# Gather of expert tokens in groups of two from tokens split once, with the activation transposes moved ahead of the weights' split

## The chip, the cores and the metric

The kernel runs on one core of one Trainium2 chip. The metric is the device time of one execution in microseconds (us). Five engines matter: TensorE (PE in the rows, its weight loads PEld), VectorE (DVE), ScalarE (ACT), GpSimd (POOL) and SyncE (SP), whose queue issues the weight transfers.

## The reference

Two decoder layers over 272 tokens (16 learned ones and 256 of the input) with a width of 1024. Each layer mixes the tokens (a gated convolution beside differential attention) and then applies a channel mixer: dense on layer 0, a mixture of eight experts on layer 1. Only the mixture is touched here:

```python
logits = einsum('bld,de->ble', h, w_router)
top_val, top_idx = lax.top_k(logits, 2)
gate = sum(one_hot(top_idx, 8) * softmax(top_val)[..., None], axis=-2)
for e in range(8):
    out = out + gate[..., e:e+1] * ((silu(h @ w_gate[e]) * (h @ w_up[e])) @ w_down[e])
h = layer_norm(ALPHA * h + out)      # ALPHA = 4 ** 0.25
```

`w_gate` and `w_up` are 1024 x 3584 for each expert, `w_down` 3584 x 1024, all float32, so the experts' weights are 352 MB.

## The kernel before, in words

**Precision.** Products are made in float32r on TensorE. Both operands are split into a float32r part `hi` and a rest `lo = x - hi`, and a product is three matmuls: hi by hi, hi by lo, lo by hi (`wmm`, lines 1020 to 1023). For the weights ScalarE writes `whi` (line 173) and VectorE `wlo` (line 174), one unit of 128 x 2048 (1 MB) at a time.

**Units and buffers.** `Weights` streams the units through raw buffers (six, and NPF = 6 more from layer 1 on; SP issues a load as soon as `wlo` has freed a buffer) and through NSPL = 4 pairs `whi`, `wlo`. `W.fill`, called behind every part (half a unit, six matmuls of 512 columns), splits the next unit when a pair has come free, so ScalarE and VectorE each get one split in every two parts, in program order with all else that they do.

**The loop.** For each of 8 experts and 7 chunks of 512 hidden columns: four gate parts (`gu_part`), the transposes of the activations of the chunk before (`act_T`, line 1038: four transposes on TensorE into a bank `t`, `aTh` on ScalarE, `aTl` on VectorE), four up parts, and four down parts for the chunk before (`down_part`). That is 12 parts, 72 matmuls, six units of weights. `silu` and `times` make the activations. The result of an expert is split (`ysplit`) and scattered to token rows (`scatter`, `scatter_add`) one chunk after its last down part, in the second chunk of the next expert.

**The gather.** Up to 128 tokens of an expert are collected by products with a 0/1 matrix `sel` (`gather_sel`, line 982). In the last chunk of each expert, `gather_k` (line 988) runs for the eight 128-row blocks k of the next expert: two float32 matmuls of 128 columns (four records in the trace, line 992) into a bank `t`, of which there are two; `xg` hi on ScalarE (line 996, with gain and bias); the same value again, `gx`, on VectorE (line 997); and the difference on GpSimd (line 998). The list `ahead` sets behind which part each block runs. The first expert's gather runs before its first parts.

**Order.** The order is written by hand: each engine runs its own instructions in program order. `act_T` stands behind the `W.fill` of the last gate part, so in the queues of ScalarE and VectorE the copies `aTh` and `aTl` stand behind `whi` and `wlo`. The bank `t` of the transposes comes free with `aTl`, and a bank of the gather with `gx`. The tiles of `aT` have four buffers, shared with `ysplit` and, at the start, with four tiles `gb` of gain and bias.

**Residual.** `residual` (line 1102) forms ALPHA * (gain * ht + bias) on GpSimd in `acc`: four multiplies of `gb` by ALPHA (line 1107) and eight `tensor_tensor` (lines 1112 and 1114), in the first chunks of the first expert.

Of the kernel before, what the change touches and what calls it, by code (L numbers as in the profile page):

```python
# [10 lines left out]
F32 = mybir.dt.float32  # L11
# [9 lines left out]
P = 128  # L21
# [9 lines left out]
NCH = DFE // 512  # L31
NRAW = 6
NSPL = 4
NPF = 6
ALPHA = 4.0 ** 0.25
EPS = 1e-5
NEG = -1e30
# [150 lines left out]
def body(tc, h0T, consts, vecs, lamv, w_in, w_out, w_gu, w_dn, w_r, mixgb, w_g, w_u, w_d, out, dbg=None):  # L188
    nc = tc.nc
    with ExitStack() as ctx:  # L190
# [763 lines left out]


        mp = ctx.enter_context(tc.tile_pool(name="moe", bufs=1))
        ht = mp.tile([P, 2, D], F32, name="ht")
        gb = [[mp.tile([P, 512], F32, tag="aT", bufs=4, name=nm("gb")) for n in range(2)] for i in range(2)]
        for i in range(2):
            for n in range(2):  # L960
# [18 lines left out]
        G = {}  # L979
        table(AF.Silu)  # L980

        def gather_sel(e):
            sel = mp.tile([P, 2, P], F32, tag="sel", bufs=1, name=nm("sel"))
            for j in range(2):
                nc.vector.tensor_scalar(sel[:, j], iota, pos[:, j, e:e + 1], None, op0=ALU.is_equal)
            G[e] = (sel, [None] * NK)

        def gather_k(e, k):
            sel, xg = G[e][:2]
            tp = bank("s", 2) if e == 0 and k % 4 > 1 else bank("t", 2)  # L990
            for j in range(2):
                nc.tensor.matmul(tp[:, 0:P], ht[:, j, k * P:(k + 1) * P], sel[:, j], start=(j == 0), stop=(j == 1))
            g, bb = vcol(V_MIX + 16 + k), vcol(V_MIX + 24 + k)
            x = mp.tile([P, P], F32, tag="gx", bufs=2, name=nm("gx"))
            xg[k] = mp.tile([P, 2, P], F32R, tag=f"xg{k}", bufs=1, name=nm("xg"))
            nc.scalar.activation(xg[k][:, 0], tp[:, 0:P], AF.Identity, scale=g, bias=bb)
            nc.vector.tensor_scalar(x, tp[:, 0:P], g, bb, op0=ALU.mult, op1=ALU.add)  # L997
            nc.gpsimd.tensor_tensor(xg[k][:, 1], x, xg[k][:, 0].bitcast(F32), ALU.subtract)  # L998

        def gather_T(e):  # L1000
            sel, xg = G[e][:2]
# [5 lines left out]
            G[e] = (sel, xg, selT)  # L1007

        def gates():
            nc.scalar.activation(ex, ex, AF.Exp)  # L1010
# [14 lines left out]
        def gu_part(o, e, p, sc=False, then=None):  # L1025

            w = W.next()
            xg = G[e][1]
            for k in range(2):
                kk = 2 * p + k  # L1030
                wmm(o, xg[kk][:, 0], xg[kk][:, 1], w.hi[:, k], w.lo[:, k], kk == 0, kk == NK - 1)
# [41 lines left out]
        def scatter(e, n, yh, yl, j):  # L1073
            o = bank("o", 1)
            for i, t in enumerate((yh, yl)):
                nc.tensor.matmul(o, G[e][2][:, j], t, start=i == 0, stop=i == 1)
            scatter_add(e, n, j, o)

        def scatter_add(e, n, j, o):
# [18 lines left out]
        def stats(j, n):  # L1098
            nc.vector.bn_stats(st[:, j, n], acc[:, j, n * 512:(n + 1) * 512])

        gather_sel(0)

        def residual():
            for i in range(2):
                for n in range(2):
                    t = gb[i][n]
                    nc.gpsimd.tensor_scalar(t, t, ALPHA, None, op0=ALU.mult)
                    for j in range(2):
                        ns = slice(n * 512, (n + 1) * 512)
                        a = acc[:, j, ns]  # L1110
                        if i == 0:
                            nc.gpsimd.tensor_tensor(a, ht[:, j, ns], t, ALU.mult)
                        else:
                            nc.gpsimd.tensor_tensor(a, a, t, ALU.add)

        ahead = ((0,), (1,), (2, 3), (4,), (5,), (6,), (7,), ())
        prev, y, pend, act = None, {}, [], None
        for e in range(NE):
            for c in range(NCH):
                end = e == NE - 1 and c == NCH - 1  # L1120
                og = bank()
                pact, act = act, mp.tile([P, 512], F32, tag="act", bufs=2, name=nm("act"))

                def silu():
# [2 lines left out]
                def on_gate(p):  # L1127
                    if e == 0 and c == 0 and p < 2:
                        for k in (4 + 2 * p, 5 + 2 * p):
                            gather_k(0, k)  # L1130
                    if p == 3:
                        silu()

                if e == 0 and c == 0:
                    for k in range(4):
                        gather_k(0, k)
                for p in range(4):
                    gu_part(og, e, p, p % 2, lambda: on_gate(p))
                if prev:
                    aT = act_T(pact)  # L1140
                    pe, pc = prev
                    if pc == 0:
                        y[pe] = [bank("s", 2) for n in range(2)]
# [2 lines left out]
                def times():  # L1146
                    nc.vector.tensor_tensor(act, act, ou, ALU.mult)

                last = c == NCH - 1 and e < NE - 1

                def then(p):
                    if p == 3:
                        times()
                    if last:
                        for k in ahead[p]:
                            gather_k(e + 1, k)

                for p in range(4):
                    gu_part(ou, e, p, p % 2, lambda: then(p))
                    if p == 3 and e < NE - 1 and c == 2:  # L1160
                        gather_sel(e + 1)
                    if p == 3 and e < NE - 1 and c == 4:
                        gather_T(e + 1)
                if end:
                    for n in range(2):
                        for p in range(2):
                            down_part(y[pe], pc, aT, n, p)
                        if n == 0:
                            aT2 = act_T(act)
                    for p in range(2):  # L1170
                        down_part(y[e], c, aT2, 0, p)
                    ys = ysplit(y[e], 0)
                    down_part(y[e], c, aT2, 1, 0)
                    for n in range(2):
                        o = [bank(), bank("o", 1)]
                        for i, j in ((0, 0), (0, 1), (1, 0), (1, 1)):
                            nc.tensor.matmul(o[j], G[e][2][:, j], ys[i], start=i == 0, stop=i == 1)
                        for j in range(2):
                            scatter_add(e, n, j, o[j])
                            if n == 1:  # L1180
                                stats(j, 1)
                                if j == 0:
                                    rstd(0)
                                    for q in ((0, 1), (1, 0), (1, 1)):
                                        final_rows(*q)
                            if n == j == 1:
                                final_scale(0)
                        if n == 0:
                            down_part(y[e], c, aT2, 1, 1)
                            stats(0, 0)  # L1190
                            ys = ysplit(y[e], 1)
                            final_rows(0, 0)
                            stats(1, 0)
                elif prev:
                    for n in range(2):
                        for p in range(2):
                            down_part(y[pe], pc, aT, n, p, (lambda: [gather_k(e + 1, k) for k in ahead[4 + 2 * n + p]]) if last else None)
# [6 lines left out]
                if e == 0 and c == 0:  # L1204
# [5 lines left out]
                if e == NE - 1 and c == NCH - 3:  # L1210
                    finb = W.take()[:, 0:2 * D].rearrange("p (a d) -> p a d", a=2)
                    xo = W.take()[:, 0:D].rearrange("p (k t) -> p k t", k=NK)


        def overflow(e):
# [5 lines left out]
            for k in range(NK):  # L1221
                tp = bank("t", 2)
                ks = slice(k * P, (k + 1) * P)
                for j in range(2):
                    nc.tensor.matmul(tp[:, :P], ht[:, j, ks], sel[:, j], start=(j == 0), stop=(j == 1))
                nc.vector.tensor_scalar(xo[:, k], tp[:, :P], vcol(V_MIX + 16 + k), vcol(V_MIX + 24 + k),
                                        op0=ALU.mult, op1=ALU.add)
# [135 lines left out]
```

## Time and profile before

| | us |
|---|---|
| median of 3 runs | 1555.19 (1549.22 to 1557.51) |
| the profiled execution | 1554.9 |
| its span in the trace | 1553.1 |
| experts' loop, first matmul of line 1021 to the last chunk's end | from 516.53 |
| a chunk without gather or scatter | 16.80 |
| a chunk with the gather of the next expert | 24.38 to 24.91, seven of them |

The span is cut into stretches at the first gate matmul of each chunk, which the timeline of TensorE shows. In a row of stretches the columns are the stretch, its length, the busy time and count of each engine, TensorE's granted clock, the share of the DMA engines and their rate. A timeline row gives start, duration, engine, line, what is written from what, and in brackets the idle time before it and what ended it.

### The profile page before, as it was taken

The page shows a single profiled execution, that of the slowest core. Times are in us where ns is not written, and L with a number is a line of the kernel's source. Part 1 is how long each engine was busy: PE and PEld are TensorE (multiplying, and loading weights), DVE is VectorE, ACT ScalarE, POOL GpSimd, SP SyncE. Part 2 cuts the span into 40 slices and gives each one's busy share as a digit, 9 for nine tenths or more (in the row PEclk, how much of TensorE's full clock was granted, in tenths as well). Part 3 has the DMA queues.
Part 4 walks back from the last instruction along what each step waited for, and adds up shares of the span by engine and source line. Part 5 has one row for each costly group of instructions (what it writes and reads, how often), then busy time and mean ns, then how long its engine had stood idle before and what let it go on. Part 6 is the DMA issues. An engine that isn't in the chain of part 4 may idle for free. (4 is left out here: it accounts for less than half of the span.)

```text
span 1553.1 us, 20974 instructions
## 1 busy us (share of the span) xinstructions
PE 1490.7 (96%) x8181; PEld 1282.5 (83%) x8181; DVE 1244.6 (80%) x1262; ACT 1007.5 (65%) x1105; POOL 134.5 (9%) x169
## 2 busy tenths in 40 slices
PE   9899999999999899999999999999999999999996
PEld 8689899999789778788788788878878878877885
DVE  8767775466866798798799798888879879888886
ACT  6655464445655767677677677767767767777773
POOL 2102200022102630000000000000000000000001
PEclk9899999999999999999999999999999999999998
DMA  8423264354527699899899889979979989997950
GB/s 304 175 82 127 92 228 154 112 189 187 192 82 291 243 358 377 306 359 374 300 358 370 345 322 369 372 295 359 371 298 358 374 316 343 376 366 300 361 207 29
DMA packets 65243, 427.99 MB, mean 276 GB/s; under 512 B 7520, under 2 KB 11616, under 8 KB 15344
## 3 DMA queue, kind: packets, MB, share of 16 engines
q1 hardware_dynamic: 64672, 426.20, 72.6%
q8 instruction: 66, 1.08, 0.3%
q10 hardware_dynamic: 432, 0.35, 0.1%
q14 instruction: 41, 0.34, 0.1%
q0 software_dynamic: 32, 0.03, 0.0%
HBM read 423.27 MB, written 1.05 MB: 273 GB/s over the span
## 5 line engine op out<-in xcount | busy, mean ns | idle before, releaser
L174 DVE TENSOR_TENSOR wlo<-raw,whi 128x2048 fp32r<-128x2048 f32 x332 | 765.8, 2309 | 116.0 <-ACT whi L173 116.0
L173 ACT ACTIVATE whi<-raw 128x2048 fp32r<-128x2048 f32 x332 | 637.8, 1921 | 185.5 <-PE ps L1023 183.9
L1021 PE MATMUL ps<-whi,xg 128*128 128x512 f32 x896 | 357.1, 398 | 0.0
L1023 PE MATMUL ps<-whi,xg 128*128 128x512 f32 x896 | 350.3, 391 | 0.2 <-POOL xg L998 0.2
L1022 PE MATMUL ps<-wlo,xg 128*128 128x512 f32 x896 | 349.6, 390 | 0.0
L284 PE MATMUL ps<-hh,whi 128*128 128x272 f32 (+4 forms) x736 | 220.1, 299 | 6.0 <-ACT hh L393 3.2
L285 PE MATMUL ps<-hl,whi 128*128 128x272 f32 (+4 forms) x736 | 216.1, 294 | 2.8 <-DVE hl L394 2.7
L287 PE MATMUL ps<-hh,wlo 128*128 128x272 f32 (+4 forms) x720 | 210.5, 292 | 2.1 <-DVE wlo L152 2.1
L152 DVE TENSOR_TENSOR wlo<-raw,whi 128x1024 fp32r<-128x1024 f32 (+2 forms) x148 | 171.2, 1179 | 36.4 <-ACT whi L145 36.3
L1023 PEld LDWEIGHTS ps<-whi,xg 128*128 128x128 f32 x896 | 168.5, 188 | 36.8 <-POOL xg L998 0.6
L1022 PEld LDWEIGHTS ps<-wlo,xg 128*128 128x128 f32 x896 | 168.8, 188 | 32.7
L1021 PEld LDWEIGHTS ps<-whi,xg 128*128 128x128 f32 x896 | 168.6, 188 | 32.4
L1021 PE MATMUL ps<-whi,aTh 128*128 128x512 f32 x448 | 177.7, 397 | 0.0
L1023 PE MATMUL ps<-whi,aTl 128*128 128x512 f32 x448 | 175.0, 391 | 2.5 <-DVE aTl L277 2.5
L145 ACT ACTIVATE whi<-raw 128x1024 fp32r<-128x1024 f32 (+2 forms) x148 | 144.9, 990 | 49.0 <-PE ps L285 37.5
L1022 PE MATMUL ps<-wlo,aTh 128*128 128x512 f32 x448 | 174.5, 389 | 0.0
L284 PEld LDWEIGHTS ps<-hh,whi 128*128 128x128 f32 x736 | 142.6, 194 | 8.6 <-ACT hh L393 3.4
L285 PEld LDWEIGHTS ps<-hl,whi 128*128 128x128 f32 x736 | 142.8, 194 | 4.7 <-DVE hl L394 3.5
L287 PEld LDWEIGHTS ps<-hh,wlo 128*128 128x128 f32 x720 | 139.1, 193 | 2.8 <-DVE wlo L152 2.8
L1023 PEld LDWEIGHTS ps<-whi,aTl 128*128 128x128 f32 x448 | 84.1, 188 | 21.5 <-DVE aTl L277 3.8
L998 POOL TENSOR_TENSOR xg<-gx,xg 128x128 fp32r<-128x128 f32 x64 | 28.6, 459 | 841.9 <-DVE gx L997 841.7
L1022 PEld LDWEIGHTS ps<-wlo,aTh 128*128 128x128 f32 x448 | 84.2, 188 | 16.3
(252 smaller groups left out, 1615.4 us busy)
## 6 DMA issues: line engine op xcount, KB each, us to landing
raw<-in_w_g_dram SPq DMA_DIRECT2D x112, 1024.0 KB, 4.9
raw<-in_w_u_dram SPq DMA_DIRECT2D x112, 1024.0 KB, 4.9
raw<-in_w_d_dram SPq DMA_DIRECT2D x112, 1024.0 KB, 4.9
raw<-in_w_in_dram SPq DMA_DIRECT2D x23, 1024.0 KB, 5.0
raw<-in_w_gu_dram SPq DMA_DIRECT2D x22, 1024.0 KB, 4.8
raw<-in_w_dn_dram SPq DMA_DIRECT2D x16, 704.0 KB, 4.1
raw<-in_w_out_dram SPq DMA_DIRECT2D x8, 1024.0 KB, 5.2
rot<-qk SPq DMA_DIRECT2D x32, 68.0 KB, 4.5
```

The source lines that it names most:

```text
L145: self.nc.scalar.activation(hi, raw, AF.Copy)
L152: self.nc.vector.tensor_tensor(lo, raw, hi.bitcast(F32), ALU.subtract)
L173: self.nc.scalar.activation(hi, raw, AF.Copy)
L174: self.nc.vector.tensor_tensor(lo, raw, hi.bitcast(F32), ALU.subtract)
L284: nc.tensor.matmul(o, w.hi[:, k], xh(k0 + k), start=first and i == 0, stop=False)
L285: nc.tensor.matmul(o, w.hi[:, k], xl(k0 + k), start=False, stop=False)
L287: nc.tensor.matmul(o, w.lo[:, k], xh(k0 + k), start=False, stop=last and i == ka - 1)
L998: nc.gpsimd.tensor_tensor(xg[k][:, 1], x, xg[k][:, 0].bitcast(F32), ALU.subtract)
L1021: nc.tensor.matmul(o, xh, whi, start=first, stop=False)
L1022: nc.tensor.matmul(o, xh, wlo, start=False, stop=False)
L1023: nc.tensor.matmul(o, xl, whi, start=False, stop=last)
```

## The change

1. `tokens_split`, once, at the end of chunk 2 of expert 0: `acc` (now gain * ht + bias, without ALPHA) is split into `xth` (ScalarE) and `xtl` (VectorE), 128 x 2048 each; then ScalarE multiplies `acc` by ALPHA in place. The four multiplies of `gb` on GpSimd are gone.
2. Experts are gathered in groups (0), (1, 2), (3, 4), (5, 6), (7). The group gather runs in the last chunk of experts 0, 2, 4 and 6, one block behind each of the eight up and down parts: four float32r matmuls (two parts by two token halves) with 256 columns (128 for the last group), hi and lo side by side in one bank, and one eviction of 128 x 512 on ScalarE. `sel` is made for the group in chunk 3.
3. `act_T` is called from the last gate part, before `silu`, before the scatter of that part and before its `W.fill`.
4. NPF is 4 instead of 6; two buffers for the end are taken a chunk later. The `xg` tiles are twice as large.

```diff
-NPF = 6
+NPF = 4
+        groups = ((0,), (1, 2), (3, 4), (5, 6), (7,))
+        def gather_sel(e):
+            n = len(group[e])
+            sel = mp.tile([P, 2, n * P], F32R, tag="selg", bufs=1, name=nm("sel"))
+            for i, ee in enumerate(group[e]):
+                for j in range(2):
+                    nc.vector.tensor_scalar(sel[:, j, i * P:(i + 1) * P], iota, pos[:, j, ee:ee + 1], None, op0=ALU.is_equal)
...
+        def tokens_split():
+            x = acc.rearrange("p j d -> p (j d)")
...
+            nc.scalar.activation(xth, x, AF.Copy)
+            nc.vector.tensor_tensor(xtl, x, xth.bitcast(F32), ALU.subtract)
+            nc.scalar.activation(x, x, AF.Copy, scale=ALPHA)
...
+        def gather_group(e, k):
+            sel, n = G["sel"], len(group[e]) * P
+            tp = bank("t", 2)
+            for i, t in enumerate(G["x"]):
+                for j in range(2):
+                    nc.tensor.matmul(tp[:, i * n:(i + 1) * n], t[:, j, k * P:(k + 1) * P], sel[:, j], start=j == 0, stop=j == 1)
+            x = G[e].xg[k] = mp.tile([P, 4 * P], F32R, tag=f"xg{k}", bufs=1, name=nm("xg"))
+            nc.scalar.activation(x[:, 0:2 * n], tp[:, 0:2 * n], AF.Copy)
...
-                    nc.gpsimd.tensor_scalar(t, t, ALPHA, None, op0=ALU.mult)
...
                     if p == 3:
+                        if prev:
+                            aT.extend(act_T(pact))
                         silu()
...
                 if prev:
-                    aT = act_T(pact)
                     pe, pc = prev
...
-                last = c == NCH - 1 and e < NE - 1
+                last = c == NCH - 1 and e + 1 in group
...
                     if last:
-                        for k in ahead[p]:
-                            gather_k(e + 1, k)
+                        gather_group(e + 1, p)
...
-                    if p == 3 and e < NE - 1 and c == 2:
+                    if p == 3 and e == 0 and c == 2:
+                        tokens_split()
+                    if p == 3 and e + 1 in group and c == 3:
                         gather_sel(e + 1)
```

## Rows read from the trace of the kernel before

**Rows 1.** The page: busy us, share of the span and instructions of each engine.

```profile
PE 1490.7 (96%) x8181; PEld 1282.5 (83%) x8181; DVE 1244.6 (80%) x1262; ACT 1007.5 (65%) x1105; POOL 134.5 (9%) x169
```

**Rows 2.** Stretches, columns as told above: chunks that hold a gather.

```profile
617.71:642.09 24.38, 21.30 (x109) 17.24 (x108) 17.74 (x16) 15.24 (x16) 3.13 (x7) 1.00 0.78 291
...
sum 171.82, PE 150.95 PEld 122.00 DVE 124.23 ACT 106.96 POOL 21.87; mean PE 21.56 PEld 17.43 DVE 17.75 ACT 15.28 POOL 3.12
```

**Rows 3.** Stretches: one expert from chunk to chunk, then single chunks.

```profile
642.09:769.56 127.47, 124.29 (x576) 102.29 (x574) 110.52 (x74) 91.26 (x66) 3.58 (x8) 1.00 0.91 346
...
548.73:566.78 18.05, 17.11 (x78) 13.83 (x76) 18.05 (x11) 12.50 (x8) 7.82 (x3) 1.00 0.91 352
...
642.09:658.89 16.80, 16.80 (x77) 13.91 (x76) 14.72 (x10) 13.00 (x9) 0.47 (x1) 1.00 0.90 345
658.89:677.56 18.67, 18.67 (x86) 15.33 (x84) 18.33 (x15) 12.97 (x9) 0.00 (x0) 1.00 0.93 348
694.37:711.16 16.79, 16.79 (x77) 13.91 (x76) 14.79 (x9) 12.51 (x8) 0.00 (x0) 1.00 0.97 375
```

**Rows 4.** Timeline of PE, ACT and DVE where a gather begins.

```profile
623.15 0.60 PE L1041 MATMUL ps<-cst,act 128*128 128x128 f32 x4
623.35 0.60 ACT L1125 ACTIVATE act<-ps 128x512 f32<-128x512 f32 x1 [0.81 <-PE ps L1023]
...
623.84 1.91 ACT L173 ACTIVATE whi<-raw 128x2048 fp32r<-128x2048 f32 x1
...
624.98 0.61 PE L992 MATMUL ps<-sel,ht 128*128 128x128 f32 x4
625.34 0.48 PE L1021 MATMUL ps<-whi,xg 128*128 128x512 f32 x1
625.65 0.59 ACT L276 ACTIVATE aTh<-ps 128x512 fp32r<-128x512 f32 x1
625.66 0.39 PE L1022 MATMUL ps<-wlo,xg 128*128 128x512 f32 x1
625.78 2.29 DVE L174 TENSOR_TENSOR wlo<-raw,whi 128x2048 fp32r<-128x2048 f32 x1 [0.91 <-ACT whi L173]
...
627.99 0.68 DVE L277 TENSOR_TENSOR aTl<-ps,aTh 128x512 fp32r<-128x512 f32 x1
628.59 0.40 DVE L997 TENSOR_SCALAR gx<-ps,vec 128x128 f32<-128x128 f32 x1
628.73 0.71 PE L992 MATMUL ps<-sel,ht 128*128 128x128 f32 x4 [1.75 <-DVE aTl L277]
```

**Rows 5.** Waits of the experts' loop: waiter, releaser, us in total, times, longest.

```profile
PE ps L992 <- DVE aTl L277: 12.3, 7, 1.8
PE ps L992 <- DVE gx L997: 8.5, 7, 1.4
PE ps L1023 <- DVE aTl L277: 2.5, 2, 1.6
ACT whi L173 <- DMA raw<-in_w_u_dram: 0.8, 1, 0.8
```

**Rows 6.** Timeline of PE: float32r matmuls of 256 columns, layer 1.

```profile
494.92 0.28 PE L287 MATMUL ps<-zh,wlo 128*128 128x256 f32 x1
...
496.34 0.28 PE L287 MATMUL ps<-zh,wlo 128*128 128x256 f32 x1
```

**Rows 7.** Groups by line, 516.53 to 566.78 us, where GpSimd forms the residual.

```profile
L174 DVE TENSOR_TENSOR wlo<-raw,whi 128x2048 fp32r<-128x2048 f32 x14 | 37.9, 2743 | 1.8 <-ACT whi L173 1.8
L1107 POOL TENSOR_SCALAR gb<-gb 128x512 f32<-128x512 f32 x4 | 12.1, 3024 | 0.0
```

**Rows 8.** Groups by line of DVE, 566.78 us to the end.

```profile
L174 DVE TENSOR_TENSOR wlo<-raw,whi 128x2048 fp32r<-128x2048 f32 x318 | 727.9, 2289 | 114.2 <-ACT whi L173 114.2
...
L985 DVE TENSOR_SCALAR sel<-cst,pos 128x128 f32<-128x128 f32 x14 | 3.3, 281 | 0.0
```

**Rows 9.** The page: DMA issues, KB each, median us from issue to landing.

```profile
raw<-in_w_u_dram SPq DMA_DIRECT2D x112, 1024.0 KB, 4.9
```

More of the change, by code (lines that the diff above doesn't have):

```diff
@@ L956, in body @@
         mp = ctx.enter_context(tc.tile_pool(name="moe", bufs=1))
-        ht = mp.tile([P, 2, D], F32, name="ht")
+        ht = mp.tile([P, 2 * D], F32, tag="ht", bufs=1, name="ht").rearrange("p (j d) -> p j d", j=2)
         gb = [[mp.tile([P, 512], F32, tag="aT", bufs=4, name=nm("gb")) for n in range(2)] for i in range(2)]
@@ L980, in body, with __init__, x, gather_first @@
         table(AF.Silu)
-        def gather_sel(e):
+        groups = ((0,), (1, 2), (3, 4), (5, 6), (7,))
+        group = {g[0]: g for g in groups}
+        class Expert:
+            def __init__(self, sel, xg, hi, lo):
+                self.sel, self.xg, self.hi, self.lo = sel, xg, slice(hi * P, hi * P + P), slice(lo * P, lo * P + P)
+            def x(self, k):
+                return self.xg[k][:, self.hi], self.xg[k][:, self.lo]
+        def gather_first():
             sel = mp.tile([P, 2, P], F32, tag="sel", bufs=1, name=nm("sel"))
@@ L984, in gather_sel @@
             for j in range(2):
[L985 to L990, printed above, removed]
+                nc.vector.tensor_scalar(sel[:, j], iota, pos[:, j, 0:1], None, op0=ALU.is_equal)
+            G[0] = Expert(sel, [None] * NK, 0, 1)
+        def gather_sel(e):
+            n = len(group[e])
+            sel = mp.tile([P, 2, n * P], F32R, tag="selg", bufs=1, name=nm("sel"))
+            xg = [None] * NK
+            for i, ee in enumerate(group[e]):
+                for j in range(2):
+                    nc.vector.tensor_scalar(sel[:, j, i * P:(i + 1) * P], iota, pos[:, j, ee:ee + 1], None, op0=ALU.is_equal)
+                G[ee] = Expert(sel[:, :, i * P:(i + 1) * P].bitcast(F32), xg, i, n + i)
+            G["sel"] = sel
@@ new lines, in tokens_split @@
+        def tokens_split():
+            x = acc.rearrange("p j d -> p (j d)")
+            xth = mp.tile([P, 2 * D], F32R, name="xth")
+            xtl = mp.tile([P, 2 * D], F32R, tag="ht", bufs=1, name="xtl")
+            nc.scalar.activation(xth, x, AF.Copy)
+            nc.vector.tensor_tensor(xtl, x, xth.bitcast(F32), ALU.subtract)
+            nc.scalar.activation(x, x, AF.Copy, scale=ALPHA)
+            G["x"] = [t.rearrange("p (j d) -> p j d", j=2) for t in (xth, xtl)]
+        def gather_group(e, k):
[6 more added lines that the diff above has]
+            nc.scalar.activation(x[:, 0:2 * n], tp[:, 0:2 * n], AF.Copy)
@@ L991, in gather_k @@
+        def gather_k(k):
+            sel, xg = G[0].sel, G[0].xg
+            tp = bank("s", 2) if k % 4 > 1 else bank("t", 2)
             for j in range(2):
@@ L994, in gather_k @@
             x = mp.tile([P, P], F32, tag="gx", bufs=2, name=nm("gx"))
-            xg[k] = mp.tile([P, 2, P], F32R, tag=f"xg{k}", bufs=1, name=nm("xg"))
-            nc.scalar.activation(xg[k][:, 0], tp[:, 0:P], AF.Identity, scale=g, bias=bb)
+            xg[k] = mp.tile([P, 4 * P], F32R, tag=f"xg{k}", bufs=1, name=nm("xg"))
+            nc.scalar.activation(xg[k][:, 0:P], tp[:, 0:P], AF.Identity, scale=g, bias=bb)
             nc.vector.tensor_scalar(x, tp[:, 0:P], g, bb, op0=ALU.mult, op1=ALU.add)
-            nc.gpsimd.tensor_tensor(xg[k][:, 1], x, xg[k][:, 0].bitcast(F32), ALU.subtract)
+            nc.gpsimd.tensor_tensor(xg[k][:, P:2 * P], x, xg[k][:, 0:P].bitcast(F32), ALU.subtract)
         def gather_T(e):
-            sel, xg = G[e][:2]
+            sel = G[e].sel
             selT = mp.tile([P, 2, P], F32R, tag="selT", bufs=2, name=nm("selT"))
@@ L1006, in gather_T @@
             nc.vector.tensor_copy(selT.rearrange("p j t -> p (j t)"), tp[:, 0:2 * P])
-            G[e] = (sel, xg, selT)
+            G[e].selT = selT
         def gates():
@@ L1027, in gu_part @@
             w = W.next()
-            xg = G[e][1]
             for k in range(2):
                 kk = 2 * p + k
-                wmm(o, xg[kk][:, 0], xg[kk][:, 1], w.hi[:, k], w.lo[:, k], kk == 0, kk == NK - 1)
+                xh, xl = G[e].x(kk)
+                wmm(o, xh, xl, w.hi[:, k], w.lo[:, k], kk == 0, kk == NK - 1)
             if then:
@@ L1075, in scatter @@
             for i, t in enumerate((yh, yl)):
-                nc.tensor.matmul(o, G[e][2][:, j], t, start=i == 0, stop=i == 1)
+                nc.tensor.matmul(o, G[e].selT[:, j], t, start=i == 0, stop=i == 1)
             scatter_add(e, n, j, o)
@@ L1099, in stats @@
             nc.vector.bn_stats(st[:, j, n], acc[:, j, n * 512:(n + 1) * 512])
-        gather_sel(0)
+        gather_first()
         def residual():
@@ L1114, in residual @@
                             nc.gpsimd.tensor_tensor(a, a, t, ALU.add)
-        ahead = ((0,), (1,), (2, 3), (4,), (5,), (6,), (7,), ())
         prev, y, pend, act = None, {}, [], None
@@ L1121, in body @@
                 og = bank()
+                aT = []
                 pact, act = act, mp.tile([P, 512], F32, tag="act", bufs=2, name=nm("act"))
@@ L1129, in on_gate @@
                         for k in (4 + 2 * p, 5 + 2 * p):
-                            gather_k(0, k)
+                            gather_k(k)
                     if p == 3:
+                        if prev:
+                            aT.extend(act_T(pact))
                         silu()
@@ L1135, in body @@
                     for k in range(4):
-                        gather_k(0, k)
+                        gather_k(k)
                 for p in range(4):
@@ L1176, in body @@
                         for i, j in ((0, 0), (0, 1), (1, 0), (1, 1)):
-                            nc.tensor.matmul(o[j], G[e][2][:, j], ys[i], start=i == 0, stop=i == 1)
+                            nc.tensor.matmul(o[j], G[e].selT[:, j], ys[i], start=i == 0, stop=i == 1)
                         for j in range(2):
@@ L1196, in body @@
                         for p in range(2):
-                            down_part(y[pe], pc, aT, n, p, (lambda: [gather_k(e + 1, k) for k in ahead[4 + 2 * n + p]]) if last else None)
+                            down_part(y[pe], pc, aT, n, p, (lambda: gather_group(e + 1, 4 + 2 * n + p)) if last else None)
                         if pc == NCH - 1:
@@ L1209, in body @@
                     nc.vector.tensor_copy(cnti[:, 0:1], cnt)
-                if e == NE - 1 and c == NCH - 3:
+                if e == NE - 1 and c == NCH - 2:
                     finb = W.take()[:, 0:2 * D].rearrange("p (a d) -> p a d", a=2)
@@ L1223, in overflow @@
                 ks = slice(k * P, (k + 1) * P)
[L1224 to L1227, printed above, removed]
+                for i, t in enumerate(G["x"]):
+                    for j in range(2):
+                        nc.tensor.matmul(tp[:, :P], t[:, j, ks].bitcast(F32), sel[:, j],
+                                         start=i == j == 0, stop=i == j == 1)
+                nc.vector.tensor_copy(xo[:, k], tp[:, :P])
             so = mp.tile([P, 2, P], F32, tag="selT", bufs=2, name=nm("oselT"))
```

## The prediction

> **What bounds the kernel now.** Begin with the busy shares of the page [rows 1]: TensorE stands at 96%, VectorE at 80%, ScalarE at 65%. Taken alone this says "TensorE", but the change touches one stage only, so cut the experts' loop into chunks and look at each one's length [rows 2, 3]. A chunk without gather or scatter takes 16.80 us, and TensorE is busy for all of it. Its 72 matmuls of 512 columns and four transposes leave (16.80 - 0.35) / 72 = 0.228 us from one matmul to the next (0.35 is the time from the transposes' start to the next matmul, 623.15 to 623.50 [rows 4]). So an ordinary chunk is bound by TensorE's own issue, and nothing that runs beside it can shorten it.
>
> The odd ones are the seven chunks that hold a gather [rows 2]: 171.82 / 7 = 24.55 us each. That is 7.75 over the plain chunk, 54.2 us in all, and it is what the change can reach. The timeline [rows 4] shows two parts in it. First, issue: the four records of a block begin at 624.98, the next matmul at 625.34, and the one behind that 0.32 later instead of 0.23, so a block takes 0.36 + 0.09 = 0.45, eight of them 3.6. Second, standstill: the second block waits 1.75 for `aTl`, which holds the bank, and `aTl` runs at 627.99 because it stands behind a `wlo` of 2.29. The waits [rows 5] give 12.3 + 8.5 = 20.8 us over seven chunks, 3.0 each, the second kind behind `gx` on VectorE. 3.6 + 3.0 = 6.6; the last 1.1 of the 7.75 are matmuls that follow each other a little slower around the blocks, and I give no cause for it.
>
> Who else is near its limit? VectorE needs 14.79 of 16.79 us in a plain chunk and 18.33 of 18.67 in the one with scatters [rows 3]. The transfers run at 375 GB/s in a plain chunk, with the DMA engines 97% busy [rows 3]. Both leave little room, and both come back below as rivals.
>
> **The change part by part.**
>
> *Three gathers go.* Experts 2, 4 and 6 are gathered with their neighbours, so three chunks fall from 24.55 to 16.80: 3 x 7.75 = -23.3. Their sixteen compares stay (0.28 each [rows 8]); four of them now stand in one chunk instead of two, 0.56 more on VectorE there, under its free 2.0 us.
>
> *Four gathers become cheaper.* A block is now four float32r matmuls of 256 columns. The nearest rows are the same shape in layer 1: twelve steps from 494.92 to 496.34, 0.118 each [rows 6]. 4 x 0.118 = 0.47; for the way back to 512 columns I add half of the 0.09 seen above, so 0.52 a block and 4.2 for eight. Bounds: 0.45 (as now) and 4 x 0.228 = 0.91 (as if each cost a 512-column one), so 3.6 to 7.3 a chunk. The last group has 128 columns; no row shows float32r there, and I take the 0.45 of the present 128-column block, the nearest one, so 3.6, with the same 7.3 as upper end. Sum: 3 x 4.2 + 3.6 = 16.2 where 4 x 7.75 = 31.0 stood: -14.8.
>
> *Where do the standstills go?* Bank `t` now comes free with the eviction on ScalarE alone, and `act_T` has passed its bank on before. Step the ScalarE queue from the gate's last matmul (0): transposes to 0.55, `aTh` to 1.15, `silu` to 1.7, `whi` to 3.6 [durations in rows 4]; the first block's sums are there at about 2.4, the second's at 4.1. An eviction of 128 x 512 from a bank costs as `aTh` does, 0.59, so the first is done by 4.2 and the second by 4.7; the third block, which needs the first bank, comes to its turn at 5.5. From then on a part with a block takes 1.37 + 0.52 = 1.9 us, two of them 3.8, and ScalarE has 1.92 + 2 x 0.59 = 3.1 to do in that time. So no standstill is left: 0, with 3.0 each (12 in all) if it came back whole. Next late behind it is nothing on VectorE, which loses its eight `gx`.
>
> *`act_T` ahead of the split, in every chunk.* TensorE's order is the same. ScalarE now runs `aTh`, `silu`, `whi`, so `whi` starts at 1.7 instead of 0.7 after the gate's last matmul, and VectorE stands at `aTl` until 1.2, then waits for `whi`; its `wlo` ends at about 6.1 instead of 4.9 (625.78 + 2.29 - 623.15). SyncE's next load, released by that `wlo`, goes out 1.2 later too. TensorE needs this unit three units later, 3 x 2.74 = 8.2. So the move is hidden by 2.1 us of lead and I cost it at nothing; without that cover it would be up to 1.2 a chunk. In the scatter chunk `aTh` also waits for the two scatter matmuls (0.45), whose operands hold its buffer; the lead there is a scatter pair longer. Bounds 0 to 1.5 for each of seven such chunks.
>
> *The start.* GpSimd loses four multiplies, 12.1 us [rows 7], and is done with the residual at about 546 instead of 556. Beside it a `wlo` takes 2.74 on average, later 2.29 [rows 7, 8], and in this stretch TensorE waits 2.5 us for `aTl` [rows 5]; VectorE is busy for the whole of chunk 2 [rows 3]. With `aTl` ahead of the `wlo`s and less of GpSimd's work I take the 2.5 back, and 0.5 of the slower matmuls there: -3.0. Lower end of the gain: 0, if `aTl` now waits for the `gb` buffers that GpSimd frees.
>
> *`tokens_split`.* Two passes of 128 x 2048 on ScalarE (1.92 each) and one on VectorE (2.29) behind the last up part of chunk 2 (0). They are chained: `whi` of the next unit to 1.9, `xth` to 3.8, `wlo` to 4.3, `xtl` to 6.5, the ALPHA pass to 8.4 because it overwrites what `xtl` reads. Queued behind it: the following `whi`, to 10.3, whose `wlo` ends at 12.6. TensorE wants that unit after four others and four transposes, 4 x 2.74 + 0.35 = 11.3. So it stands about 1.5, and I take 2 with what the gates' small steps of chunk 3 add. Bounds 0 to 5 (everything that it puts on VectorE and ScalarE, less what the lead hides). Net of the start: -1.0.
>
> *NPF 4.* A raw buffer goes round in 12 units, 12 x 2.8 = 33.6 us; of it landing takes 4.9 [rows 9] and the two splits 6. With ten buffers 28.0 - 11 = 17 us are left to wait. One wait of 0.8 us on a load in the whole loop [rows 5] fits that. Nothing, then.
>
> *Sum.* -23.3 - 14.8 - 1.0 = -39.1. On the profiled execution (1554.9) that is **1516 us**; the three runs have their median 0.3 above it, so no correction.
>
> **The rivals.**
>
> *The transfers become the bound.* Over a whole expert they moved 346 GB/s [rows 3], and the gather chunk is where they rest (DMA share 0.72 to 0.78 [rows 2]). Two experts without a gather between them ask for 88.1 MB in about 244 us, 361 GB/s. If 346 were all that can be had, the whole gain would be lost: 1555. Half way, at 353, some 1535. Against it: single chunks run at 375 [rows 3], landing stays at 4.9 us, and one load in 336 was waited for.
>
> The Trainium skill has a rule that speaks for this rival: DMA: Bandwidth & Descriptors, section "Where 436 GB/s comes from", puts the limit of HBM for a core at about 358 GB/s. By that rule a two-expert period would be 246 us instead of 244, an estimate of 8 us over the whole loop, 1524. The chunk at 375 GB/s contradicts it for a core that runs alone.
>
> *The evictions hold TensorE.* If ScalarE's queue lets each bank go late, four chunks keep their 3.0 us of standstill or more: with the present 7.75 in all four, 1555 - 23.3 - 1 = 1531.
>
> *Slower: the split falls behind.* The place is VectorE's queue at the gate's end, where it now waits for `aTh` and then for `whi`. If those 1.2 us cannot be made up in the free 2.0 of a chunk, each of 55 chunks gets longer by them: 1516 + 66 = 1582. It decides where `wlo` ends later than 8.2 us after its pair came free; I count 6.1.
>
> *It doesn't do what it says:* blocks cost 0.91 and the start's gain fails. 16.2 becomes 29.2, the start +2: 1516 + 13 + 3 = 1532.
>
> **How the numbers follow.** My forecast has a chance of 0.77, evictions and dearer blocks together 0.11, the transfers 0.06 (half of it at 1535, half near 1555), the slower case 0.04, something unseen that undoes the gain 0.02. The forecast's own bounds: -4 (blocks at 0.45, the start's whole gain, no stall at the split) to +8 (a third of the dearer blocks, 3 more at the start), and the runs before lie between 6 below and 2 above their median. That gives **1508 to 1530**; evictions at 1531 are just outside. A difference under 0.5% is about what a measurement of this kernel cannot tell from none, 7.8 us; all but the worst cases are beyond it: faster 0.92, same 0.04, slower 0.04.
>
> **What the profile of the changed kernel would show.** The chunks between experts 1 and 2, 3 and 4, 5 and 6 at 16.8 us; the four others at about 21.0, with no wait of the gather's matmuls on VectorE; the plain chunk still at 16.80; one wait of TensorE for `wlo` of about 2 us in chunk 3 of the first expert; the DMA rate near 375 GB/s over a dozen chunks with landing under 8 us. I am wrong if plain chunks grow, if ScalarE waits for loads, or if the group's blocks step by more than 0.6.

## The result, and the profile after

| | before | after |
|---|---|---|
| median, us | 1555.15 (1549.22 to 1557.51, 4 runs) | 1519.57 (1512.47 to 1521.10, 4 runs) |
| the profiled execution, its span | 1554.9, 1553.1 | 1521.1, 1519.3 |
| the loop, first gate matmul to the start of the last chunk | 516.53 to 1510.08: 993.55 | 519.31 to 1476.36: 957.05 |

The ratio of the times is 0.9758 with a 95% interval of 0.9735 to 0.9781. The forecast was 1516, the range 1508 to 1530. The median fell by 35.6 us, the span by 33.8. Of the span, the loop gives -36.5, and +2.8 arose before the loop, where the change alters nothing but the number of raw buffers; the last chunk and the end give -0.1.

The page of the kernel after: busy time, share and instructions of each engine, and one line of the DMA issues. It answers to [rows 1, 9].

```profile
PE 1478.9 (97%) x8085; PEld 1277.9 (84%) x8085; DVE 1221.0 (80%) x1207; ACT 1000.0 (66%) x1083; POOL 100.9 (7%) x109
...
raw<-in_w_u_dram SPq DMA_DIRECT2D x112, 1024.0 KB, 7.2
```

The shares hardly moved. What moved is in the stretches, cut as in [rows 2, 3]: the first two chunks together, chunks 2 to 5 of expert 0, its chunk 6 with the gather for experts 1 and 2, then the last chunk of expert 1 (no gather any more), and two of the three other chunks with a gather. The last row is the whole loop.

```profile
519.31:550.29 30.98, 30.68 (x145) 24.74 (x144) 27.32 (x22) 22.25 (x20) 25.85 (x16) 1.00 0.62 219
550.29:567.70 17.41, 17.16 (x77) 13.76 (x76) 17.41 (x11) 12.27 (x8) 0.00 (x0) 1.00 0.97 371
567.70:588.79 21.09, 18.93 (x77) 15.07 (x76) 17.31 (x12) 15.84 (x10) 0.00 (x0) 0.92 0.82 317
588.79:605.84 17.05, 17.05 (x80) 14.08 (x78) 16.14 (x19) 15.14 (x12) 0.00 (x0) 1.00 0.99 372
605.84:622.61 16.77, 16.77 (x77) 13.92 (x76) 15.45 (x11) 12.39 (x8) 0.00 (x0) 1.00 0.96 380
622.61:643.38 20.77, 20.77 (x110) 17.72 (x109) 15.48 (x9) 15.88 (x15) 0.00 (x0) 1.00 0.96 367
...
746.36:763.18 16.82, 16.82 (x78) 13.90 (x77) 14.74 (x9) 12.38 (x8) 0.00 (x0) 1.00 0.96 364
...
1109.63:1130.40 20.77, 20.77 (x109) 17.73 (x108) 15.48 (x9) 15.89 (x15) 0.00 (x0) 1.00 0.98 371
1353.14:1373.54 20.40, 20.40 (x109) 17.43 (x108) 15.62 (x9) 14.37 (x15) 0.00 (x0) 1.00 0.94 378
...
519.31:1476.36 957.05, 954.34 (x4372) 789.23 (x4371) 844.08 (x520) 706.88 (x496) 25.85 (x16) 1.00 0.93 355
```

Read the first and second column of each row, then compare the length with TensorE's busy time. In the four gather chunks the two are equal: no standstill is left. They take 20.77 three times and 20.40 once, the three chunks that lost their gather 16.81 to 16.82, together 133.2 where [rows 2] have 171.8: -38.7. TensorE still stands in the first chunks (0.30) and in chunk 2 (0.25), and for long only in chunk 3, where 21.09 stands beside 18.93, at a granted clock of 0.92. That chunk took 16.81 before. So the change has a price, 4.3 us, and it sits in the chunk behind `tokens_split`.

The sum by chunks: gathers -38.7; first two chunks 32.20 to 30.98, -1.2; chunk 2, 18.05 [rows 3] to 17.41, -0.6; chunk 3, +4.3; chunk 4, 17.34 to 17.05, -0.3. That makes -36.5, the loop's difference.

The timeline of PE, ACT and DVE where a gather begins, answering to [rows 4]:

```profile
628.69 0.60 ACT L276 ACTIVATE aTh<-ps 128x512 fp32r<-128x512 f32 x1 [1.23 <-PE ps L1084]
...
629.70 0.68 DVE L277 TENSOR_TENSOR aTl<-ps,aTh 128x512 fp32r<-128x512 f32 x1
...
629.88 0.40 PE L1027 MATMUL ps<-sel,xth 128*128 128x256 f32 x2
630.12 0.41 PE L1027 MATMUL ps<-sel,xtl 128*128 128x256 f32 x2
630.36 0.40 PE L1064 MATMUL ps<-whi,xg 128*128 128x512 f32 x1
```

The four records of a block run from 629.88 to 630.36, so a block takes 0.48, and nothing in it carries a wait.

Now chunk 3, where the time came back. The waits of TensorE in the loop (waiter, releaser, total, times, longest), to be held against [rows 5]:

```profile
PE ps L1065 <- DVE wlo L174: 2.1, 2, 1.8
PE ps L1064 <- ACT whi L173: 0.3, 1, 0.3
```

And the timeline of the same kernel through that stretch:

```profile
562.04 0.39 PE L1066 MATMUL ps<-whi,xg 128*128 128x512 f32 x1
...
562.46 1.93 ACT L173 ACTIVATE whi<-raw 128x2048 fp32r<-128x2048 f32 x1 [0.72 <-PE ps L1066]
564.30 1.90 ACT L1016 ACTIVATE xth<-h 128x2048 fp32r<-128x2048 f32 x1
565.20 0.68 DVE L1190 TENSOR_TENSOR act<-act,ps 128x512 f32<-128x512 f32 x1
565.80 2.28 DVE L174 TENSOR_TENSOR wlo<-raw,whi 128x2048 fp32r<-128x2048 f32 x1
568.00 2.28 DVE L1017 TENSOR_TENSOR xtl<-h,xth 128x2048 fp32r<-128x2048 f32 x1
570.32 1.92 ACT L1018 ACTIVATE h<-h 128x2048 f32<-128x2048 f32 x1 [4.12 <-DVE xtl L1017]
572.14 5.49 ACT L173 ACTIVATE whi<-raw 128x2048 fp32r<-128x2048 f32 x3
...
574.07 4.49 DVE L174 TENSOR_TENSOR wlo<-raw,whi 128x2048 fp32r<-128x2048 f32 x2 [3.78 <-ACT whi L173]
574.09 0.50 PE L1064 MATMUL ps<-whi,xg 128*128 128x512 f32 x1 [0.34 <-ACT whi L173]
...
576.41 0.50 PE L1065 MATMUL ps<-wlo,xg 128*128 128x512 f32 x1 [1.82 <-DVE wlo L174]
...
577.80 0.63 PE L1066 MATMUL ps<-whi,xg 128*128 128x512 f32 x1
578.23 0.63 PE L1064 MATMUL ps<-whi,xg 128*128 128x512 f32 x1
```

Follow the brackets. The first line is the last up matmul of chunk 2. ScalarE is through with `xth` at 566.2 and then stands 4.12 us, because the next instruction in its queue, the ALPHA pass, overwrites what `xtl` reads. VectorE does not come to `xtl` before 568.00. The next unit's `whi` stands behind the ALPHA pass and starts at 572.14; its `wlo` waits 3.78 for it, and TensorE waits 0.34 and 1.82 for the pair. The last two lines show a second loss: from one matmul to the next it is 0.43 instead of 0.227.

The same as a stretch of that kernel, the standstill's end to the last slow matmul:

```profile
576.90:580.40 3.50, 3.50 (x11) 2.68 (x10) 3.50 (x2) 3.50 (x4) 0.00 (x0) 0.52 0.83 300
```

The granted clock is 0.52 here, the level of 1.2 GHz, and what TensorE did before it was to stand for 2.2 us within 2.7. Nine matmuls 0.2 apart too far make another 1.8. 2.2 + 1.8 is all but 0.3 of the 4.3.

### The profile page after: what moved, and what is told of

Its sections match the earlier page's. It is cut to its first block, busy times and chain, and to the rows that moved or that the text cites. A ratio compares the mean times of both kernels' runs of the same rounds, so it can differ in the third digit from the quotient of the medians.

```text
span 1519.3 us, 20543 instructions
## 1 busy us (share of the span) xinstructions
PE 1478.9 (97%) x8085; PEld 1277.9 (84%) x8085; DVE 1221.0 (80%) x1207; ACT 1000.0 (66%) x1083; POOL 100.9 (7%) x109
## 5 line engine op out<-in xcount | busy, mean ns | idle before, releaser
L174 DVE TENSOR_TENSOR wlo<-raw,whi 128x2048 fp32r<-128x2048 f32 x332 | 758.2, 2305 | 112.7 <-ACT whi L173 110.9
L1064 PEld LDWEIGHTS ps<-whi,aTh 128*128 128x128 f32 x448 | 84.2, 188 | 16.9
```

Source lines behind the costliest of these rows:

```text
L174: self.nc.vector.tensor_tensor(lo, raw, hi.bitcast(F32), ALU.subtract)
L1064: nc.tensor.matmul(o, xh, whi, start=first, stop=False)
```

## The experiments

Each kernel is the kernel after with one edit, except in "What is the move worth in the kernel before?", where the edit is made on the kernel before. "Loop" is the time from the first gate matmul to the start of the last chunk, 993.55 before and 957.05 after. It is the better yardstick: it starts between 510.9 and 520.5 us in the profiles of this study, and that spread has nothing to do with the edits.

**Is it the ALPHA pass that holds chunk 3?** The pass is moved two chunks later.

```diff
-            nc.scalar.activation(x, x, AF.Copy, scale=ALPHA)
             G["x"] = [t.rearrange("p (j d) -> p j d", j=2) for t in (xth, xtl)]
...
+        def alpha_pass():
+            x = acc.rearrange("p j d -> p (j d)")
+            nc.scalar.activation(x, x, AF.Copy, scale=ALPHA)
...
+                    if p == 3 and e == 0 and c == 4:
+                        alpha_pass()
```

> Edit: of the token split at the end of chunk 2 of expert 0, the in-place pass by ALPHA on ScalarE alone is moved to the end of chunk 4. Theory: it is this pass that holds ScalarE's queue in chunk 3 (it waits 4.1 us for xtl, and the next whi stands behind it). Without it the next whi is done at about 568 and its wlo, behind xtl, at 572.5, before TensorE wants them at 573.5. Then the two waits (0.34 and 1.82 us) go, and with them the stretch of slow matmuls behind them: chunk 3 falls from 21.09 to 16.8 to 17.1 us, the kernel by 4 us. Rival: the wait comes from VectorE alone, which is late from the residual's time and gets 2.3 us of xtl on top. Then TensorE still waits about 2 us for wlo in chunk 3, and the chunk stays above 20.

Measured: 1515.20 in one run, loop 952.56, 4.5 less than after. Chunk 3 of this kernel:

```profile
566.01:582.82 16.81, 16.81 (x77) 13.90 (x76) 16.81 (x10) 12.58 (x9) 0.00 (x0) 1.00 0.98 383
```

Chunk 3 is a plain chunk again, with VectorE busy for all of it; `xth` and `xtl` are still made there. VectorE is as late here as in the kernel after: `times` starts 3.15 us after the last up matmul of chunk 2 does (560.34 and 563.49). The pass costs nothing at its new place either, chunk 5 takes 16.8. So without the ALPHA pass behind `xtl` there is no price: the rival, VectorE's lateness alone, falls, and the split of the tokens by itself costs nothing.

**Is it the chain, or the backlog from GpSimd's work?** First `tokens_split`, with its ALPHA pass, two chunks later, where the residual is long done.

```diff
-                    if p == 3 and e == 0 and c == 2:
+                    if p == 3 and e == 0 and c == 4:
                         tokens_split()
```

> Edit: the token split, ALPHA pass included, at the end of chunk 4 of expert 0 instead of chunk 2, where VectorE is no longer late from the residual. Theory (chain plus backlog): the chain alone, as the prediction stepped it, puts the wlo that TensorE wants 1.0 to 1.5 us late, so chunk 5 is 17.8 to 18.4 us, or up to 20 if TensorE's clock falls behind the standstill; chunk 3 is 16.8. Rival (backlog alone): with VectorE on time the chain is hidden by the lead, chunk 5 stays at 16.8, and the kernel is as fast as with the late ALPHA pass, about 4 us below the changed one.

Measured: 1519.30 in one run, loop 957.46. Chunk 3 takes 16.82, and chunk 5, the one behind the split:

```profile
600.02:620.80 20.78, 18.95 (x77) 15.07 (x76) 17.33 (x12) 15.87 (x10) 0.00 (x0) 0.92 0.77 302
```

One wait of 1.82 for `wlo`, the same granted clock of 0.92, 4.0 us over the 16.77 of this chunk in the kernel after, where the theory allowed 20 at most. The standstill moved with the split, and GpSimd's work just before it is not needed. But the edit did not put VectorE on time, as its theory and its rival both took for granted. The last up matmul of chunk 4, `times` on VectorE, and the standstill of this kernel:

```profile
594.11 0.39 PE L1066 MATMUL ps<-whi,xg 128*128 128x512 f32 x1
...
597.19 0.68 DVE L1190 TENSOR_TENSOR act<-act,ps 128x512 f32<-128x512 f32 x1
...
608.40 0.70 PE L1065 MATMUL ps<-wlo,xg 128*128 128x512 f32 x1 [1.82 <-DVE wlo L174]
```

`times` starts 3.1 us after the last up matmul does. In the kernel after it was 3.2 (562.04 and 565.20, above). In chunk 4 VectorE has seven small operations for the gates' weights; whether they alone make it late no run shows. So this run does not tell the chain from the backlog; the next one does.

Then the other way round: the residual's eight operations on GpSimd are left out (`acc` is zero), so that no `wlo` of the first chunks is slowed.

```diff
-            for i in range(2):
-                for n in range(2):
...
+            nc.gpsimd.memset(acc.rearrange("p j d -> p (j d)"), 0.0)
```

> Edit: the eight products and sums of the residual on GpSimd are left out; it only sets acc to zero, so the residual and the tokens of experts 1 to 7 are missing from the result. Theory: VectorE is late at the token split because each wlo beside the residual takes 2.7 to 3.2 us instead of 2.29. Without the residual all wlo of the first chunks take 2.29, chunk 2 is 16.8, and the wait in chunk 3 shrinks from 2.2 to about 1.3 us, without the slow matmuls behind it: chunk 3 at 18.0. Rival: the wlo are slow for another reason (transfers, the banks) and stay at 2.7, and chunk 3 stays at 21.

Measured: 1510.11 in one run, loop 953.71. Chunks 2 and 3 of this kernel:

```profile
541.71:558.50 16.79, 16.79 (x77) 13.91 (x76) 14.69 (x9) 12.27 (x8) 0.00 (x0) 1.00 0.95 351
558.50:577.11 18.61, 17.04 (x77) 13.90 (x76) 14.82 (x9) 15.62 (x10) 0.00 (x0) 1.00 0.82 320
```

TensorE stands 1.57 us in chunk 3, close to the 1.5 that the prediction gave for the bare chain (this theory had 1.3, and 18.0 for the chunk). The clock stays at 1.00, and the chunk is 1.8 over a plain one, not 4.3. Chunk 2 is plain too. VectorE is less late here, 2.3 us from the start of the last up matmul of chunk 2 to `times`:

```profile
552.84 0.39 PE L1066 MATMUL ps<-whi,xg 128*128 128x512 f32 x1
...
555.13 0.68 DVE L1181 TENSOR_TENSOR act<-act,ps 128x512 f32<-128x512 f32 x1
...
566.35 0.50 PE L1065 MATMUL ps<-wlo,xg 128*128 128x512 f32 x1 [1.57 <-DVE wlo L174]
```

So the four kernels sort themselves. With VectorE late but the ALPHA pass elsewhere (the first experiment) nothing is lost; with the chain and VectorE at 2.3 the loss is 1.8; with the chain and VectorE at 3.1 or 3.2 it is 4.0 to 4.3. The pass is needed for a standstill, and a later VectorE goes with a longer one, behind which the clock falls. The later split and this kernel have one profile each; chunk 3 of the kernel after takes 21.09 again in a second one.

Beside the stretches, the groups by line of VectorE in the first chunks, to be held against the 2743 ns of [rows 7]: first the kernel after,

```profile
L174 DVE TENSOR_TENSOR wlo<-raw,whi 128x2048 fp32r<-128x2048 f32 x14 | 37.0, 2674 | 1.4 <-ACT whi L173 1.3
```

then this kernel without the residual:

```profile
L174 DVE TENSOR_TENSOR wlo<-raw,whi 128x2048 fp32r<-128x2048 f32 x16 | 36.3, 2290 | 9.0 <-ACT whi L173 9.0
```

In the first chunks a `wlo` takes 2.67 us on average with GpSimd's `tensor_tensor` work beside some of them, and 2.29 without it: that is the backlog of chunk 2, and the rival, another reason for the slow `wlo`, falls.

**Did the move of `act_T` take the standstills out of the gather chunks?** It is put back behind the split of the weights.

```diff
                     if p == 3:
-                        if prev:
-                            aT.extend(act_T(pact))
                         silu()
...
                 if prev:
+                    aT.extend(act_T(pact))
                     pe, pc = prev
```

> Edit: the changed kernel with act_T back behind the split, where it was. Theory: the move ahead is worth only what it frees in the gather chunks and at the start: the first gather block again waits 1.7 us for aTl in the four gather chunks (20.77 to about 22.5, the last 20.40 to 22.1, 7 us in all), up to 2.5 us come back in chunks 1 and 2 of expert 0, and plain chunks stay at 16.80: 7 to 9 us slower than the changed kernel. Rival: group gather with one eviction has enough slack by itself; the gather chunks stay at 20.8 and the kernel within 2 us of the changed one.

Measured: 1521.38 in one run, loop 960.89, 3.8 more than after. The first two chunks, chunk 3 and the first gather chunk of this kernel:

```profile
515.90:552.23 36.33, 33.05 (x145) 26.89 (x144) 31.02 (x25) 22.15 (x19) 25.85 (x16) 0.92 0.66 232
...
569.02:588.88 19.86, 17.37 (x77) 13.83 (x76) 16.07 (x11) 15.61 (x10) 0.00 (x0) 1.00 0.74 272
...
623.01:643.81 20.80, 20.80 (x109) 17.66 (x108) 15.49 (x9) 15.89 (x15) 0.00 (x0) 1.00 0.93 345
```

The gather chunk is unchanged, so the theory fell here. Its timeline tells why:

```profile
631.43 0.60 ACT L1029 ACTIVATE xg<-ps 128x512 fp32r<-128x512 f32 x1
...
632.08 0.30 PEld L1027 LDWEIGHTS ps<-sel,xth 128*128 128x128 f32 x2 [0.20 <-ACT xg L1029]
632.15 0.45 PE L1027 MATMUL ps<-sel,xth 128*128 128x256 f32 x2
...
633.31 0.68 DVE L277 TENSOR_TENSOR aTl<-ps,aTh 128x512 fp32r<-128x512 f32 x1
```

The second block goes at 632.15, just behind the eviction of the first (631.43 + 0.60), and long before `aTl` has left its bank at 633.99. So it takes the first block's bank, which comes free first; what sets this choice no run shows. In the kernel before both banks came free on VectorE, `aTl` and then `gx` [rows 4], so both stood behind `wlo`; now one of them comes free on ScalarE, and that suffices. The move pays elsewhere, in the first two chunks: without it they take 36.33 instead of 30.98, with one standstill of 3.3 for `aTl`, and matmuls at the lower clock behind it. Part of this is given back, since chunk 2 takes 16.79 and chunk 3 19.86 here.

**What is the move worth in the kernel before?** Only that edit, on the kernel before.

```diff
+                aT = []
...
                     if p == 3:
+                        if prev:
+                            aT.extend(act_T(pact))
                         silu()
...
                 if prev:
-                    aT = act_T(pact)
```

> Edit: the kernel before with one part of the change alone, act_T ahead of the split. Theory: the wait for aTl (12.3 us over the seven gather chunks, 2.5 at the start) goes, the wait for gx stays: gather chunks at about 22.8 instead of 24.55, chunks 1 and 2 of expert 0 shorter by 2 in all, 1540 to 1543. Rival: gx on VectorE, queued behind the same wlo, takes the place of aTl as what holds the bank; the gather chunks stay near 24.5 and the kernel at about 1552.

Measured: 1543.04 in one run, loop 977.71, 15.8 less than before. The seven gather chunks take 22.37 to 22.80, 157.6 in all, 14.2 less than in [rows 2]. One of them, and then what TensorE waits for in the loop of this kernel:

```profile
745.35:767.84 22.49, 21.34 (x110) 17.25 (x108) 17.76 (x16) 15.47 (x16) 5.26 (x7) 1.00 0.85 319
```

```profile
PE ps L992 <- DVE gx L997: 8.1, 14, 0.9
```

The wait for `aTl` is gone, and two shorter waits for `gx` a chunk are left, 1.16 in all. So the move alone gets two of the 7.75 us. Of the 5.7 that are left, 1.16 are these waits, and TensorE is busy for the rest: 21.34 stands against 16.80 in a plain chunk, for the blocks themselves and the slower steps around them.

**What does gathering for two at a time bring?** Groups of one expert, all else as after.

```diff
-        groups = ((0,), (1, 2), (3, 4), (5, 6), (7,))
+        groups = tuple((i,) for i in range(NE))
```

> Edit: the changed kernel with groups of one expert, so seven gathers of 128 columns from the split tokens. Theory: a gather chunk costs TensorE's issue alone, as the last one of the changed kernel does (20.40, 3.6 above a plain chunk): 7 x 3.6 = 25.2 us in place of 15.5, so 9.7 us slower than the changed kernel, about 1529, and still some 26 faster than the kernel before. Rival: the gain comes from the pairs; single gathers meet the waits of before, a chunk costs about 24, and the kernel stands at 1550 or above.

Measured: 1530.72 in one run, loop 967.02, 10.0 more than after, where three chunks are 3.6 longer and three 0.4 shorter (9.7 was expected). All seven gather chunks look like this:

```profile
622.12:642.52 20.40, 20.40 (x110) 17.42 (x108) 15.61 (x9) 14.39 (x15) 0.00 (x0) 1.00 0.97 374
```

A block of 128 columns costs nearly what one of 256 costs, 3.6 against 4.0 a chunk, so two experts are gathered almost for the price of one.

**Do the transfers hold the loop?** NPF, the raw buffers that are added from layer 1 on, goes from 4 to 2.

```diff
-NPF = 4
+NPF = 2
```

> Edit: two raw buffers less once more (NPF 2 for 4, eight in all). Theory: landing takes 7.3 us in the changed kernel; a buffer goes round in 8 x 2.8 = 22.4 us, of which landing and the two splits take 7.3 + 6, so 9 us are left and nothing waits: plain chunks 16.80, the loop within 1 us of the changed kernel. Rival (the transfers are at their limit and live from the lead): ScalarE waits for loads, plain chunks grow past 17 us, and the kernel loses 10 us or more.

Measured: 1522.06 in one run. The loop of this kernel:

```profile
520.31:1477.35 957.04, 954.26 (x4371) 789.11 (x4370) 844.07 (x520) 706.51 (x496) 25.86 (x16) 1.00 0.95 357
```

In this loop neither TensorE nor ScalarE nor VectorE waits for a load; in the loop of the kernel after VectorE does once, for 1.4. The loop takes 957.04, as with four. Two buffers fewer change nothing, so the loads come early enough with eight as with ten. How far the rate of the transfers is from its limit this edit does not test; in both kernels no standstill of TensorE in the loop ends with a load.

**The better version, timed.** The kernel of the first experiment, and the unedited kernel after beside it on the same chip.

> The kernel with the late ALPHA pass again, timed. Theory: 4.3 us below the changed kernel, 1515 to 1516, ratio to before 0.973. Rival: what chunk 3 gives back is lost in another place, 1519 to 1520, ratio 0.976.

> The changed kernel, unedited, on the same chip as the one with the late ALPHA pass. Theory: 1519 to 1520, ratio to before 0.976, above the other by about 4 us. Its stretch before the experts' loop, which the change does not touch, should differ from run to run by up to 3 us, as it did in the profiles so far (515.9 to 520.4).

| | median, us | ratio to before, 95% interval | loop |
|---|---|---|---|
| ALPHA pass late | 1513.04 (1507.74 to 1517.16) | 0.9744 (0.9717 to 0.9772) | 953.48 |
| after | 1520.59 (1510.92 to 1522.38) | 0.9776 (0.9747 to 0.9806) | 957.09 |

Chunk 3 takes 16.79 in the one and 21.09 in the other, as in the earlier profiles. The loop is 3.6 shorter, and that repeats; the whole times' intervals overlap. Of the 7.5 us between the medians only about 4 belong to the edit: the stretch before the loop was 511.3 in the one profile and 520.5 in the other, where 3 were expected at most, though both kernels are the same up to there.

## Why the prediction was right, point by point

**What bounds the kernel: right.** Plain chunks take 16.77 to 16.86 through all edits, where they took 16.77 to 16.81 before [rows 3]. Time came only from chunks in which TensorE stood or ran the gather.

**Three gathers go: right.** -23.3 was counted and -23.2 measured (3 x 24.55 to 50.4).

**Four gathers become cheaper: the sum right, one reason wrong.** 16.2 was counted for the four and 15.5 measured (82.7 less four plain chunks). The step that took 0.52 for a block from the layer's 256-column matmuls [rows 6] holds: 0.48. The step on the standstills named two reasons, the eviction on ScalarE alone "and `act_T` has passed its bank on before". The second is not needed: with `act_T` back behind the split the chunk is 20.80. The step took the second block to need the bank of the transposes; in that trace it gets the first block's, which comes free earlier.

**`act_T` ahead of the split, at nothing: right for plain chunks, and too little elsewhere.** No plain chunk grew by more than 0.1, and the scatter chunks, bounded at 0 to 1.5, take 18.72 to 18.75 where 18.67 to 18.71 stood, so the rival in which VectorE falls behind by 1.2 a chunk (1582) fell. The move brings 3.8 in the loop after, at the start, where the prediction had put 2.5 + 0.5 for it and GpSimd's work together. In the kernel before the same move brings 15.8, of which 14.2 lie in the gather chunks. The parts of this change are not additive: in the kernel after, the gather chunks gain nothing by the move.

**The start: right in sign, sized 3.0, measured 2.1** (1.2 + 0.6 + 0.3, in chunks 0 to 4 without chunk 3). In the first chunks a `wlo` still takes 2.67 us on average, because eight `tensor_tensor` operations stayed and only the four multiplies went. The Trainium skill, page SBUF — State Buffer, section "Who interferes with whom", says that a VectorE instruction with two SBUF inputs contends with a GpSimd instruction that reads SBUF. The 2.67 against 2.29 agrees with it.

**`tokens_split`: the mechanism right, the term mis-sized.** 2 was counted, 4.3 measured. The chain was counted link by link. Its terms give 12.6 - 11.3 = 1.3, which the prediction called about 1.5, and the kernel without the residual shows 1.57. Two things were missing. The backlog: the prediction had VectorE free for the split as in a plain chunk, but `times`, ahead of it in the queue, starts 3.2 us after the last up matmul, not 2.3 as without the residual, and TensorE stands for 2.2. And above all the clock: nine matmuls at 0.43 behind the standstill, 1.8 more. The bounds of 0 to 5 held it, in part by luck, because they were drawn from the work of VectorE and ScalarE and have no term for the clock. Where the split is moved to chunk 4, VectorE is late as well (3.1), the standstill is 1.82, and the lower clock follows. No run has the 4 us with VectorE at 2.3.

**The sum.** -39.1 was forecast, and the loop gave -36.5: 2.3 more for the split, 0.9 less at the start, 0.6 more gained at the gathers. The other 2.8 on the profiled execution lie before the loop. No run ties them to the change: in kernels that are alike up to there that stretch took from 510.9 to 520.5, and the 516.5 of before lies between.

**The rivals.** The transfers: after the change they move 355 GB/s over the loop where it was 340, 380 in a plain chunk, and landing takes 7.2 us instead of 4.9 [rows 9]; TensorE and ScalarE wait for none in the loop, VectorE once for 1.4, and fewer buffers change nothing. The Trainium skill, page DMA: Bandwidth & Descriptors, section "Where 436 GB/s comes from", puts HBM's limit for a core at about 358 GB/s; the chunks at 371 to 380 contradict it for a core that runs alone. The evictions do not hold TensorE, and a block steps by 0.48, not 0.91: both other rivals fell in the four gather chunks.

## What to carry to other kernels

When an engine's queue holds an instruction that must wait for another engine, count what is queued behind it, and put it where it waits for nothing: a pass that was needed only much later, moved by two chunks, gave back 4 us. A buffer is passed on by its slowest reader, so evict with one engine, the one that is not in backlog. And cost two parts of a change on top of each other, not each on the kernel before: one edit here was worth 15.8 alone and 3.8 beside the others. Before an experiment is said to separate two causes, look in its trace whether the one is really gone: moving the split left VectorE as late as before.

## What was not expected of the hardware

A standstill of TensorE can cost about twice its length. The granted clock fell to about 0.5 (1.2 GHz), with matmuls 0.43 apart, behind standstills of 2.2 us in chunk 3 of the kernel after, 1.82 in chunk 5 of the kernel with the later split and 3.3 in the first chunks of the one with `act_T` back. Chunk 3 shows the same in the three other profiles in which the split stands as in the kernel after and `act_T` is ahead of it (21.09 to 21.13). It did not fall behind 1.57 without the residual, nor behind 1.59 in the first chunks of the kernel before, nor behind 1.25 and 1.24 in chunk 3 of the kernel with `act_T` back. In the kernel before it fell in one of the seven gather chunks, which all stand for 1.75 once:

```profile
1000.00:1024.91 24.91, 22.95 (x109) 18.51 (x108) 17.74 (x16) 15.48 (x16) 3.13 (x7) 0.93 0.75 275
```

So nearly equal standstills go either way, and the runs don't tell what decides between them.

The stretch before the loop differs from one execution to another by up to 9.6 us, in kernels that are the same up to there, and with it the granted clock of single stretches. From 80 to 120 us it was 0.87 in the kernel after and 1.00 in the timed one with the late ALPHA pass, here as two stretches:

```profile
80.00:120.00 40.00, 39.47 (x241) 32.89 (x241) 22.25 (x62) 19.74 (x66) 0.40 (x4) 0.87 0.23 80
```

```profile
80.00:120.00 40.00, 39.47 (x276) 33.14 (x275) 25.76 (x68) 21.43 (x71) 0.40 (x4) 1.00 0.27 103
```

The granted clock over the whole stretch before the loop goes with its length: 0.97 in the two profiles with 510.9 and 511.3, 0.96 in the four from 515.9 to 517.8, 0.95 in the five from 518.8 to 520.5. One and the same kernel, the one with the late ALPHA pass, had 517.8 in its first profile and 511.3 in its second. Why the clock differs stays open. This spread is why a difference of 4 us was read from chunks and not from whole times.
